# A hybrid decoder trunk: the normalized operands move to another pool, and every attention score product contracts over all 128 partitions

## The chip, the cores and the metric

The kernel runs on one core of one Trainium2 chip. The metric is the device time of one execution in microseconds. Three executions of the kernel before the change gave a median of 1401.86 us, with 1396.67 us the lowest and 1404.54 us the highest.

## What is computed

Two transformer-like layers work on 512 tokens of width 1024. Layer 0 projects its input with one weight matrix for two groups of heads: four retention heads (RetNet) and eight sparse attention heads (NSA) in two key/value groups. The attention has a compressed branch (31 compressed keys), a selected branch and a window branch. With 512 tokens there are eight blocks of 64 tokens and eight are selected, and the window is 512, so both of the latter see every earlier token. Layer 1 is a gated linear recurrence (HGRN2). Each layer ends with a SwiGLU feed-forward network of width 2816. The part that the change touches is cut from the reference here:

```python
def block(i):
    ...
    s_c = jnp.einsum('bghqd,bgnd->bghqn', qb, k_cmp) * scale
    p_c = masked_softmax(s_c, cmp_end[None, :] <= t[:, None])
    ...
    s_s = jnp.einsum('bghqd,bgqkd->bghqk', qb, kg) * scale
    p_s = masked_softmax(s_s, (kpos <= t[None, None, :, None])[:, :, None])
    ...
    s_w = jnp.einsum('bghqd,bgkd->bghqk', qb, kw) * scale
    o_w = jnp.einsum('bghqk,bgkd->bghqd', masked_softmax(s_w, valid_w), vw)

for layer in range(DEPTH):
    h = rmsnorm(x, norm_mix_g[layer])
    ...
    h = rmsnorm(x, norm_ffn_g[layer])
    x = x + swiglu(h, ffn_w1[layer], ffn_w3[layer], ffn_w2[layer]).astype(x.dtype)
```

## The kernel before

**Operands in two parts.** Activations lie feature-major: 128 features on the partitions, 512 tokens along the row. A float32 operand is split into a high and a low part of type float32r, and a product is the sum of three: high by high, low by high, high by low. `accumulate` (L121) issues these three as L127, L128 and L129. The weights are split by `load_split` (L104): a DMA brings a raw block, ScalarE casts the high part `whi`, VectorE or GpSimd subtracts for the low part `wlo`. Both sit in the pool `wp`. The norm writes its result as `hh` (high) and `hl` (low), eight tiles of 128 by 512 each (`Norm.operand`, L166), which lie in the pool `main`. Every projection streams `hh` and `hl` past the weights: the tiles `p_a` and `p_b` of the feed-forward networks, `p_r`, `p_rg`, `p_nq` and others in layer 0, `p_hf`, `p_hq`, `p_hi`, `p_hg` in layer 1. The second half of a feed-forward network (tile `y`) streams `gh` and `gl`, which lie in the pool `big`; so do the operands of the output projections (tile `mo`).

**Attention.** For a head, the query tile `QA` holds the high part on the 64 partitions of its group and the low part on the other 64. The key's high part is kept on both halves (`KA`), so one product over 128 rows (L443) gives high by high plus low by high. The key's low part lies in `KB` only on the group's own 64 partitions, and a second product over these 64 rows (L444) adds high by low. A third, of bf16 (L445), adds the causal mask:

```python
mm(s_[:, 0:n], QA[g][t][:, qs], KA[:, 2 * br + g, 0:n], start=True, stop=False)
mm(s_[:, 0:n], QA[g][t][b, qs], KB[br][b, 0:n], start=False, stop=False)
mm(s_[:, qs], identb, cmaskb, start=False, stop=True)
```

Here `b` is the group's half and `n` is 128, 256, 384 or 512, by the block of queries. There are 64 such triples. The compressed branch does the same with 32 columns (L400 with `kca`, L401 with `kcb` over 64 rows), 32 pairs in four runs of eight (function `nsa`). VectorE then takes the row maximum from PSUM (L446), ScalarE the exponential (L449), GpSimd scales (L456), TensorE transposes (L466), ScalarE and VectorE split the result, and TensorE multiplies by the values (L473, L474).

**Order.** The steps of the attention and of the retention heads are put in one list by `weave` (L56), so that projections `p_r` stand between the attention's products, and scores are issued two steps ahead of the values that use them. The framework's scheduler then settles the order on each engine; each engine runs its own instructions in that order and waits for semaphores.

Of the kernel before, what the change touches and what calls it, by code (L numbers as in the profile page):

```python
# [11 lines left out]
F32 = mybir.dt.float32  # L12
FR = mybir.dt.float32r
# [3 lines left out]
ALU = mybir.AluOpType  # L17
# [3 lines left out]
S = 512  # L21
D = 1024
KT = D // 128
# [8 lines left out]
def trunk(ctx, tc, t_in, out):  # L32
# [22 lines left out]
    # Sequences of steps (matrix time, step) in one, each spread evenly over a span of the whole.  # L55
# [12 lines left out]
    # Residual stream, feature-major.  # L68
    xall = main.tile([128, KT, S], F32, name="xall")
    xT = [xall[:, k, :] for k in range(KT)]  # L70
    hh = [main.tile([128, S], FR, name=f"hh{k}") for k in range(KT)]
    hl = [main.tile([128, S], FR, name=f"hl{k}") for k in range(KT)]
# [28 lines left out]
    # Weights: one block of K-tiles, split exactly into two float32r parts.  # L101
# [35 lines left out]
    # The same in four steps, the last of which hands the sums on.  # L137
# [17 lines left out]
    # RMSNorm: operands x*g; the row factor is applied where products are read.  # L155
# [97 lines left out]
    # ---------------------------------------------------------------- layer 0  # L253
    n0 = Norm(0)
    w0 = t_in["w_in0"]
    # Attention operands in two float32r parts. Per head, a query's halves lie on the two halves
    # of the partitions, beside a key's high part twice; a value's halves lie side by side.
# [3 lines left out]
    KB = [cell(4 + br, f"kb{br}", FR) for br in range(2)]  # L261
# [30 lines left out]
    # kc, vc with token pairs on the partitions: [(j2, d), group, token]  # L292
# [7 lines left out]
    for br in range(2):  # L300
        kf = temp(f"kf{br}")
        nc.vector.tensor_tensor(out=kf, in0=first[2 + br], in1=R0, op=ALU.mult)
        for g in range(2):
            b = slice(g * 64, g * 64 + 64)
            ka = KA[:, 2 * br + g, :]
            for h in range(2):
                nc.scalar.copy(ka[h * 64:h * 64 + 64], kf[b])
            nc.vector.tensor_tensor(out=KB[br][b], in0=kf[b], in1=ka[b].bitcast(F32), op=ALU.subtract)
# [12 lines left out]
    # Compressed keys and values.  # L321
    kca = main.tile([128, 2, 32], FR, name="kca")
    kcb = main.tile([128, 32], FR, name="kcb")
    vc = main.tile([96, 2, 128], FR, name="vc")
    for z in (kca.rearrange("p g n -> p (g n)"), kcb, vc.rearrange("p g d -> p (g d)")):
        nc.scalar.activation(out=z, in_=ones[:z.shape[0], 0:1].to_broadcast(list(z.shape)), func=AF.Copy, scale=0.0)
    for s in range(2):
# [22 lines left out]
        if s == 0:  # L350
            mm(po[:, 0:62], cw2[:, 0:128], u, start=True, stop=True)
            for g in range(2):
                b, src = slice(g * 64, g * 64 + 64), po[:, g * 31:g * 31 + 31]
                nc.scalar.copy(kca[:, g, 0:31], src)
                nc.vector.tensor_tensor(out=kcb[b, 0:31], in0=src[b], in1=kca[b, g, 0:31].bitcast(F32),
                                        op=ALU.subtract)
        else:
            for g in range(2):
                mm(po[:31, g * 64:g * 64 + 64], u[:, g * 31:g * 31 + 31], cw2[:, 128:192], start=True, stop=True)
            src = po[:31, 0:128].rearrange("p (g d) -> p g d", g=2)  # L360
            for r in (0, 32):
                nc.scalar.copy(vc[r:r + 31, :, 0:64], src)
            nc.vector.tensor_tensor(out=vc[64:95, :, 0:64], in0=src, in1=vc[0:31, :, 0:64].bitcast(F32),
                                    op=ALU.subtract)
# [21 lines left out]
    # NSA attention.  # L386
# [3 lines left out]
    def nsa(i):  # L390
# [4 lines left out]
        for g in range(2):  # L395
            b = slice(g * 64, g * 64 + 64)
            sc = bank("sc", f"sc{i}_{g}")
            for t in range(4):
                o = sc[:, t * 32:t * 32 + 32]
                mm(o, QA[g][t][:, qs], kca[:, g, :], start=True, stop=False)  # L400
                mm(o, QA[g][t][b, qs], kcb[b, :], start=False, stop=True)  # L401
            nc.vector.tensor_tensor(out=pc[:, g * 4:g * 4 + 4, 0:31],
                                    in0=sc[:, 0:128].rearrange("p (h n) -> p h n", h=4)[:, :, 0:31],
                                    in1=cmpmask[:, i:i + 1, 0:31].to_broadcast([128, 4, 31]), op=ALU.add)
# [28 lines left out]
    def nsa_scores(i, g, tp, br):  # L433
        n = (i + 1) * 128
        qs = slice(i * 128, n)
        b = slice(g * 64, g * 64 + 64)
        st = small.tile([128, 8], F32, name=f"st{i}_{g}{tp}_{br}", tag="st", bufs=4)
        Ps = []
        for x in range(2):
# [4 lines left out]
            mm(s_[:, 0:n], QA[g][t][b, qs], KB[br][b, 0:n], start=False, stop=False)  # L444
# [37 lines left out]
    # Steps of two heads and a branch; later steps' scores run ahead of a step's values.  # L482
# [27 lines left out]
    # RetNet.  # L510
# [126 lines left out]
    # ---------------------------------------------------------------- layer 1  # L637
# [7 lines left out]
    # Lower bound of the forget gate: a running sum of a softmax over the odd layers, less its  # L645
    # first term, over the single odd layer.
# [45 lines left out]
    def hgrn_mix(h):  # L692
# [6 lines left out]
        # Products over d of a token with itself and with its nearest neighbours, summed by ones.  # L699
# [83 lines left out]
        # The scale of q, 1/sqrt(128), is taken into eps: o is sqrt(128) times the reference's.  # L783
# [24 lines left out]
    # Projections in order, one a beat; each head's recurrence runs beside the next heads'.  # L808
# [44 lines left out]
def _layout(i):  # L853
# [37 lines left out]
    # Constants of the shapes.  # L891
# [34 lines left out]
```

## Time and profile before

The profiled execution spans 1400.5 us from its first to its last instruction, 1.4 us below the median of the three timed ones.

| What | Before |
|---|---|
| median of 3 executions | 1401.86 us |
| span of the profiled execution | 1400.5 us |
| TensorE (PE) busy | 1378.0 us, 98% |
| VectorE (DVE) busy | 718.9 us, 51% |
| ScalarE (ACT) busy | 529.3 us, 38% |
| GpSimd (POOL) busy | 375.5 us, 27% |
| mean granted TensorE clock | 0.985 of full |
| HBM traffic | 83 GB/s over the span |

How to read it: a busy share counts the time in which at least one instruction of the engine is under way. Products on TensorE overlap, since one begins while the one before it still drains, so a product's own duration is longer than the time it costs. What it costs is the distance from its start to the next one's start.

### The profile page before, as it was taken

Reading aid. Unit: us, or ns where it says so; the run is one execution under the profiler, and the core shown is the slowest. Engines: PE = TensorE matmul, PEld = TensorE weight load, DVE = VectorE, ACT = ScalarE, POOL = GpSimd, SP = SyncE. Lnnn points to the kernel's source line nnn. Section 1 sums busy time; section 2 is a strip of 40 time slices with the busy share of each in tenths; the row PEclk is TensorE's granted clock in tenths of the full one; section 3 lists DMA queues with packets and bytes.
Section 4 is the critical chain, followed back from the end, with each engine's and each line's share of the span. In section 5 each row is a group of like instructions: output and inputs, shape, how many; then the busy total and the mean of one; then the engine's idle time right before and its main releaser. Section 6 shows DMA issues by size and latency. Waiting matters only on the chain.

```text
span 1400.5 us, 17591 instructions
## 1 busy us (share of the span) xinstructions
PE 1378.0 (98%) x6591; PEld 1120.4 (80%) x6591; DVE 718.9 (51%) x1261; ACT 529.3 (38%) x982; POOL 375.5 (27%) x383
## 2 busy tenths in 40 slices
PE   7999999999999999999999999999999999999996
PEld 5777778788888888888888888888788888888886
DVE  5744575675343334443438877775743433334333
ACT  5444564644333322333434333332433322233342
POOL 3013556532111000111118656661211110011112
PEclk9998899999999999999999999999999999999998
DMA  6231011103233234333332222222233323323332
GB/s 217 76 91 46 31 31 32 45 18 115 81 102 92 83 100 134 90 91 92 97 98 76 76 61 61 74 62 69 82 92 92 103 83 97 107 92 90 87 91 79
DMA packets 38774, 116.71 MB, mean 83 GB/s; under 512 B 4833, under 2 KB 11169, under 8 KB 38561
## 3 DMA queue, kind: packets, MB, share of 16 engines
q1 hardware_dynamic: 38688, 115.58, 27.6%
q8 instruction: 52, 0.85, 0.3%
q14 instruction: 34, 0.27, 0.1%
HBM read 113.47 MB, written 2.10 MB: 83 GB/s over the span
## 4 chain that ended last, share of the span: by engine, by line
PE 97%; DVE 1%; issue 0%; ACT 0%; DMA 0%; POOL 0%; SPq 0%; DVEq 0%; ACTq 0%; POOLq 0%
PE p_b L129 6%; PE p_b L127 6%; PE p_a L128 6%; PE p_a L127 6%; PE p_b L128 6%; PE p_a L129 6%; PE y L127 6%; PE y L128 6%; PE y L129 6%; PE mo L127 2%; PE mo L128 2%; PE lv L741 2%; PE mo L129 2%; PE p_r L127 2%; PE p_r L128 2%; PE p_r L129 2%
## 5 line engine op out<-in xcount | busy, mean ns | idle before, releaser
L248 POOL TENSOR_TENSOR g<-g,R 128x512 f32<-128x512 f32 x44 | 70.2, 1596 | 535.0 <-DVE g L247 525.4
L129 PE MATMUL p_b<-hh,wlo_b 128*128 128x512 f32 x352 | 139.7, 397 | 0.0
L127 PE MATMUL p_a<-hh,whi_a 128*128 128x512 f32 x352 | 139.7, 397 | 0.0
L127 PE MATMUL p_b<-hh,whi_b 128*128 128x512 f32 x352 | 139.7, 397 | 0.0
L128 PE MATMUL p_a<-hl,whi_a 128*128 128x512 f32 x352 | 139.7, 397 | 0.0
L128 PE MATMUL p_b<-hl,whi_b 128*128 128x512 f32 x352 | 139.5, 396 | 0.0
L129 PE MATMUL p_a<-hh,wlo_a 128*128 128x512 f32 x352 | 139.5, 396 | 0.0
L127 PE MATMUL y<-gh,whi_y 128*128 128x512 f32 (+1 forms) x363 | 139.0, 383 | 0.4 <-DVE xall L223 0.4
L128 PE MATMUL y<-gl,whi_y 128*128 128x512 f32 (+1 forms) x363 | 138.3, 383 | 0.0
L129 PE MATMUL y<-gh,wlo_y 128*128 128x512 f32 (+1 forms) x363 | 138.2, 383 | 0.0
L116 DVE TENSOR_TENSOR wlo_y<-raw_y,whi_y 128x512 fp32r<-128x512 f32 (+1 forms) x96 | 62.6, 653 | 95.2 <-ACT whi_y L114 95.2
L114 ACT CAST whi_y<-raw_y 128x512 fp32r<-128x512 f32 (+1 forms) x96 | 56.4, 587 | 145.8 <-PE y L128 101.9
L116 DVE TENSOR_TENSOR wlo_b<-raw_b,whi_b 128x512 fp32r<-128x512 f32 x88 | 62.7, 713 | 92.8 <-ACT whi_b L114 92.7
L114 ACT CAST whi_b<-raw_b 128x512 fp32r<-128x512 f32 x88 | 54.8, 622 | 135.6 <-issue 61.9
L114 ACT CAST whi_a<-raw_a 128x512 fp32r<-128x512 f32 x88 | 54.6, 620 | 104.5 <-PE p_b L128 71.9
L180 POOL TENSOR_TENSOR acc<-acc,sq 128x512 f32<-128x512 f32 x30 | 41.8, 1394 | 151.9 <-ACT sq L179 151.3
L127 PEld LDWEIGHTS y<-gh,whi_y 128*128 128x128 f32 x363 | 68.2, 188 | 13.9 <-DVE xall L223 0.5
L129 PEld LDWEIGHTS p_a<-hh,wlo_a 128*128 128x128 f32 x352 | 66.3, 188 | 16.1
L129 PEld LDWEIGHTS p_b<-hh,wlo_b 128*128 128x128 f32 x352 | 66.3, 188 | 16.1
L128 PEld LDWEIGHTS p_b<-hl,whi_b 128*128 128x128 f32 x352 | 66.3, 188 | 16.1
L127 PEld LDWEIGHTS p_b<-hh,whi_b 128*128 128x128 f32 x352 | 66.3, 188 | 16.0
L128 PEld LDWEIGHTS p_a<-hl,whi_a 128*128 128x128 f32 x352 | 66.3, 188 | 16.0
(364 smaller groups left out, 3111.7 us busy)
## 6 DMA issues: line engine op xcount, KB each, us to landing
raw_a<-w SPq DMA_DIRECT2D x44, 512.0 KB, 3.6
raw_b<-w SPq DMA_DIRECT2D x44, 512.0 KB, 3.6
raw_y<-w SPq DMA_DIRECT2D x32, 512.0 KB, 3.5
raw_mo<-w_out SPq DMA_DIRECT2D x16, 512.0 KB, 3.6
raw_r<-w_in SPq DMA_DIRECT2D x12, 512.0 KB, 3.7
raw_y<-w SPq DMA_DIRECT2D x32, 192.0 KB, 2.4
raw_hf<-w_in SPq DMA_DIRECT2D x8, 512.0 KB, 3.6
raw_hq<-w_in SPq DMA_DIRECT2D x8, 512.0 KB, 3.6
```

The source lines that it names most:

```text
L114: nc.scalar.copy(hi[:, :m], part)
L116: lo_eng[c // 512 % len(lo_eng)].tensor_tensor(out=lo[:, :m], in0=part, in1=hi[:, :m].bitcast(F32), op=ALU.subtract)
L127: mm(o, wh, xh, start=first and j == 0, stop=False)
L128: mm(o, wh, xl, start=False, stop=False)
L129: mm(o, wl, xh, start=False, stop=last and j == n - 1)
L180: nc.gpsimd.tensor_tensor(out=self.acc, in0=self.acc, in1=sq, op=ALU.add)
L248: nc.gpsimd.tensor_tensor(out=g, in0=g, in1=R, op=ALU.mult)
L741: mm(s_[:M, c * 64:(c + 1) * 64].rearrange("p (a b) -> p a b", b=B), k[:, c * 128:c * 128 + M], q4[:, c * nb:(c + 1) * nb, 1, :], start=Tr ...
```

## The change

`hh` and `hl` are allocated from the pool `wp`, ahead of the weights' tiles, with one buffer each. `KB` becomes one slab of four 128 by 512 tiles (one for each branch and group), filled on both halves of the partitions by four subtractions for a branch instead of two; `kcb` likewise gets one 128-row tile for each group. L444 and L401 then contract over all 128 rows, and so add low by low as well. The scratch that the framework keeps at the start of each partition for DMA descriptors shrinks from 16384 to 4096 bytes. Comments are dropped, so lines shift by one to four: L400 and L401 become L403 and L404, L443 to L445 become L445 to L447, L308 becomes L310, L127 to L129 become L128 to L130.

```diff
-    hh = [main.tile([128, S], FR, name=f"hh{k}") for k in range(KT)]
-    hl = [main.tile([128, S], FR, name=f"hl{k}") for k in range(KT)]
+    hh = [wp.tile([128, S], FR, name=f"hh{k}", tag=f"hh{k}", bufs=1) for k in range(KT)]
+    hl = [wp.tile([128, S], FR, name=f"hl{k}", tag=f"hl{k}", bufs=1) for k in range(KT)]
...
-    KB = [cell(4 + br, f"kb{br}", FR) for br in range(2)]
+    KB = slab(4, "kb", FR)
...
-            nc.vector.tensor_tensor(out=KB[br][b], in0=kf[b], in1=ka[b].bitcast(F32), op=ALU.subtract)
+            for h in range(2):
+                nc.vector.tensor_tensor(out=KB[h * 64:h * 64 + 64, 2 * br + g, :], in0=kf[b],
+                                        in1=ka[b].bitcast(F32), op=ALU.subtract)
...
-    kcb = main.tile([128, 32], FR, name="kcb")
+    kcb = main.tile([128, 2, 32], FR, name="kcb")
...
-                nc.vector.tensor_tensor(out=kcb[b, 0:31], in0=src[b], in1=kca[b, g, 0:31].bitcast(F32),
+                nc.vector.tensor_tensor(out=kcb[:, g, 0:31], in0=src, in1=kca[:, g, 0:31].bitcast(F32),
                                         op=ALU.subtract)
...
-                mm(o, QA[g][t][b, qs], kcb[b, :], start=False, stop=True)
+                mm(o, QA[g][t][:, qs], kcb[:, g, :], start=False, stop=True)
...
-            mm(s_[:, 0:n], QA[g][t][b, qs], KB[br][b, 0:n], start=False, stop=False)
+            mm(s_[:, 0:n], QA[g][t][:, qs], KB[:, 2 * br + g, 0:n], start=False, stop=False)
...
-    nc = _bacc.Bacc("TRN2", target_bir_lowering=False, num_devices=1)
+    nc = _bacc.Bacc("TRN2", target_bir_lowering=False, num_devices=1, dynamic_dma_scratch_size=4096)
```

The pools lie one behind the other in each partition, so tiles of different pools need not start on the same grid. In the two programs as built, the first tile of a kind starts at this byte of the partition (tiles of a kind follow at multiples of 2048):

| Tile | Before | Rest by 64 | After | Rest by 64 |
|---|---|---|---|---|
| `hh` | 32896 | 0 | 31072 | 32 |
| `whi`, `wlo` | 76000 | 32 | 63840 | 32 |
| `gh`, `gl` (first slab) | 121056 | 32 | 108896 | 32 |

The order on SP and GpSimd stays the same. On the other engines it moves in one place, where layer 0's keys and values are made. On VectorE, before (`kb` is the keys' low part, `vf` a value projection ahead of its transposes, `vv` the values' two parts, `wlo_nq` a low part of weights):

```order
L308 TENSOR_TENSOR kb_144<-kf_377,ka 64x512 x2
L308 TENSOR_TENSOR kb_145<-kf_385,ka 64x512
L313 TENSOR_TENSOR vf_428<-p_v_393,R_279 128x512
L308 TENSOR_TENSOR kb_145<-kf_385,ka 64x512
L116 TENSOR_TENSOR wlo_nq_0_608<-raw_nq_604,whi_nq_0_606 128x512
L116 TENSOR_TENSOR wlo_nq_512_612<-raw_nq_604,whi_nq_512_610 128x512
L116 TENSOR_TENSOR wlo_nq_0_649<-raw_nq_645,whi_nq_0_647 128x512
L313 TENSOR_TENSOR vf_472<-p_v_437,R_279 128x512
```

The same place on VectorE in the changed kernel:

```order
L310 TENSOR_TENSOR kb<-kf_376,ka 64x512 x4
L310 TENSOR_TENSOR kb<-kf_386,ka 64x512 x2
L316 TENSOR_TENSOR vf_431<-p_v_396,R_278 128x512
L310 TENSOR_TENSOR kb<-kf_386,ka 64x512 x2
L117 TENSOR_TENSOR wlo_nq_0_611<-raw_nq_607,whi_nq_0_609 128x512
L117 TENSOR_TENSOR wlo_nq_512_615<-raw_nq_607,whi_nq_512_613 128x512
L117 TENSOR_TENSOR wlo_nq_0_652<-raw_nq_648,whi_nq_0_650 128x512
L316 TENSOR_TENSOR vf_475<-p_v_440,R_278 128x512
```

Three more subtractions stand ahead of the first `vf`, and four more ahead of the second.

On TensorE at the same place, before (`h` is the compressed keys' first layer, `vt` the transposes of `vf`):

```order
L338 MATMUL h_0_487<-xkv_488,cw_0_154 64x62 x4
L316 MATMUL vt_430<-ident,vf_428 128x128 x4
L338 MATMUL h_0_487<-xkv_488,cw_0_154 64x62 x4
L338 MATMUL h_0_487<-xkv_499,cw_1_155 64x62 x6
L316 MATMUL vt_474<-ident,vf_472 128x128 x4
```

The same place on TensorE in the changed kernel:

```order
L342 MATMUL h_0_490<-xkv_491,cw_0_153 64x62 x8
L342 MATMUL h_0_490<-xkv_502,cw_1_154 64x62
L319 MATMUL vt_433<-ident,vf_431 128x128 x4
L342 MATMUL h_0_490<-xkv_502,cw_1_154 64x62 x7
L128 MATMUL p_ng<-hh_74,whi_ng_569 32x512
```

The first group of transposes stands five products later, and the second 25 products later: behind the last two of `h` and 23 of the 24 products of `p_ng`.

## Rows read from the trace of the kernel before

**Rows 1.** The page: busy time of each engine, and the chain that ended last.
```profile
PE 1378.0 (98%) x6591; PEld 1120.4 (80%) x6591; DVE 718.9 (51%) x1261; ACT 529.3 (38%) x982; POOL 375.5 (27%) x383
PE 97%; DVE 1%; issue 0%; ACT 0%; DMA 0%; POOL 0%; SPq 0%; DVEq 0%; ACTq 0%; POOLq 0%
```

**Rows 2.** Sums by stretch: stretch, its us, busy us of engines, clock, DMA share, GB/s.
```profile
534.92:658.62 123.70, 123.70 (x530) 99.45 (x528) 50.53 (x77) 39.45 (x65) 16.03 (x10) 1.00 0.32 95
475.06:534.92 59.86, 59.86 (x265) 49.56 (x264) 21.07 (x33) 14.78 (x26) 1.62 (x1) 1.00 0.37 112
```

**Rows 3.** The same view, whole span, instructions on hh alone, then on hl alone.
```profile
0.00:1401.00 1401.00, 762.76 (x2352) 444.27 (x2352) 30.30 (x32) 23.11 (x32) 0.99 0.28 83
0.00:1401.00 1401.00, 471.95 (x1176) 222.92 (x1176) 30.30 (x32) 0.99 0.28 83
```

**Rows 4.** One line's instructions, L444 and L401: count, duration, first and last start.
```profile
L444 PE MATMUL s<-kb,qa x64: 322/438/686, 111.1 to 291.3; 64*128 64x128 f32 x16, 64*128 64x256 f32 x16, 64*128 64x384 f32 x16, 64*128 64x512 f32 x16
...
L401 PE MATMUL sc<-kcb,qa x32: 280/280/393, 107.4 to 220.2; 64*128 64x32 f32 x32
```

**Rows 5.** Waits: engine, line, released by: us in total, times, longest us.
```profile
PEld s L444 <- issue: 10.2, 42, 0.4
```

**Rows 6.** Timeline of TensorE: start, us, instruction; a score triple at n = 512.
```profile
272.41 0.48 PE L443 MATMUL s<-ka,qa 128*128 128x512 f32 x1
272.82 0.49 PE L444 MATMUL s<-kb,qa 64*128 64x512 f32 x1
273.25 0.23 PE L445 MATMUL s<-cmaskb,identb 128*128 128x128 bf16 x1
```

**Rows 7.** Timeline of TensorE, a score triple at n = 128.
```profile
123.59 0.30 PE L443 MATMUL s<-ka,qa 128*128 128x128 f32 x1
123.82 0.32 PE L444 MATMUL s<-kb,qa 64*128 64x128 f32 x1
124.08 0.23 PE L445 MATMUL s<-cmaskb,identb 128*128 128x128 bf16 x1
```

**Rows 8.** Timeline of TensorE, products over all rows behind the mask, and four transposes.
```profile
118.81 0.23 PE L445 MATMUL s<-cmaskb,identb 128*128 128x128 bf16 x1
118.85 0.48 PE L128 MATMUL p_r<-hl,whi_r 128*128 128x512 f32 x1
119.16 0.22 PE L443 MATMUL s<-ka,qa 128*128 128x128 f32 x1
...
285.58 0.60 PE L466 MATMUL pt<-ident,P 128*128 128x128 f32 x4
285.94 0.48 PE L443 MATMUL s<-ka,qa 128*128 128x512 f32 x1
```

**Rows 9.** Timeline of TensorE, the compressed branch's narrow products.
```profile
171.53 0.28 PE L401 MATMUL sc<-kcb,qa 64*128 64x32 f32 x1
171.74 0.28 PE L400 MATMUL sc<-kca,qa 128*128 128x32 f32 x1
171.95 0.28 PE L401 MATMUL sc<-kcb,qa 64*128 64x32 f32 x1
```

**Rows 10.** Sums by stretch: three at the lower clock, and the whole attention stage.
```profile
110.36:117.19 6.83, 6.83 (x20) 5.12 (x20) 2.27 (x8) 1.35 (x4) 0.00 (x0) 0.50 0.00 0
134.26:147.91 13.65, 13.65 (x49) 10.85 (x49) 7.41 (x27) 5.62 (x19) 4.53 (x8) 0.50 0.01 2
219.59:226.42 6.83, 6.83 (x24) 5.61 (x24) 3.97 (x13) 2.22 (x7) 3.19 (x4) 0.50 0.00 0
107.00:296.00 189.00, 188.42 (x990) 146.87 (x989) 114.46 (x294) 100.75 (x250) 95.12 (x106) 0.93 0.12 37
```

**Rows 11.** The chain that ended last, in order of time, where it leaves TensorE: start, us.
```profile
272.95 1.03 DVE st L454
...
274.12 1.05 POOL P L456
275.17 0.56 issue
```

**Rows 12.** One line's instructions, L308: count, shortest/median/longest ns, first and last start.
```profile
L308 DVE TENSOR_TENSOR kb<-kf,ka x4: 669/686/690, 46.1 to 48.8; 64x512 fp32r<-64x512 f32 x4
```

More of the change, by code (lines that the diff above doesn't have):

```diff
@@ L322, in trunk @@
     kca = main.tile([128, 2, 32], FR, name="kca")
-    kcb = main.tile([128, 32], FR, name="kcb")
+    kcb = main.tile([128, 2, 32], FR, name="kcb")
     vc = main.tile([96, 2, 128], FR, name="vc")
-    for z in (kca.rearrange("p g n -> p (g n)"), kcb, vc.rearrange("p g d -> p (g d)")):
+    for z in (kca.rearrange("p g n -> p (g n)"), kcb.rearrange("p g n -> p (g n)"),
+              vc.rearrange("p g d -> p (g d)")):
         nc.scalar.activation(out=z, in_=ones[:z.shape[0], 0:1].to_broadcast(list(z.shape)), func=AF.Copy, scale=0.0)
@@ L352, in trunk @@
             for g in range(2):
-                b, src = slice(g * 64, g * 64 + 64), po[:, g * 31:g * 31 + 31]
+                src = po[:, g * 31:g * 31 + 31]
                 nc.scalar.copy(kca[:, g, 0:31], src)
-                nc.vector.tensor_tensor(out=kcb[b, 0:31], in0=src[b], in1=kca[b, g, 0:31].bitcast(F32),
+                nc.vector.tensor_tensor(out=kcb[:, g, 0:31], in0=src, in1=kca[:, g, 0:31].bitcast(F32),
                                         op=ALU.subtract)
@@ L395, in nsa @@
         for g in range(2):
-            b = slice(g * 64, g * 64 + 64)
             sc = bank("sc", f"sc{i}_{g}")
@@ L435, in nsa_scores @@
         qs = slice(i * 128, n)
-        b = slice(g * 64, g * 64 + 64)
         st = small.tile([128, 8], F32, name=f"st{i}_{g}{tp}_{br}", tag="st", bufs=4)
```

## The prediction

> **What bounds the kernel now.** I read the page first: TensorE is busy 98% of the span and the chain that ended last runs through it for 97% [rows 1]. Every other engine has idle time, so a change pays where it shortens the distance from one product's start to the next one's, or takes a wait from TensorE. The next view is the one of sums by stretch, because busy shares cannot show what a product costs. The second half of the first feed-forward network has a pure stretch of `p_a`/`p_b`, whose moving operands are `hh` and `hl`, and the first half ends with a pure stretch of `y`, which streams `gh` and `gl`. Counted by weight loads (one for each product), the first has 528 products in 123.70 us, 234.3 ns each, and the second 264 in 59.86 us, 226.7 ns each [rows 2]. All are 128 by 512 products over 128 rows, at the full clock and without a gap; DMA moves 95 and 112 GB/s, so the faster stretch has more traffic, not less. Something about `hh` and `hl` costs 7.5 ns a product. In the attention stage I read the timeline. A score triple at 512 columns has its starts at 272.41, 272.82 and 273.25: the 128-row L443 takes 0.41 us to the next start and the 64-row L444 takes 0.43 [rows 6], where a plain product of that size takes 0.23. At 128 columns the same two take 0.23 and 0.26 [rows 7], while four transposes of 128 columns take 0.36, or 0.09 each [rows 8]. The weight load of L444 is the one that the view of waits lists as held, 10.2 us over 42 times, with no releaser named [rows 5]: it does not slip under the product before it, as the others do. Last I looked at the clock: three stretches of 6.83, 13.65 and 6.83 us have a granted clock of 0.50, 1.2 GHz instead of 2.4 [rows 10]. Each begins within a run of the compressed branch's narrow products or right at its end; the last of these starts is at 220.2 [rows 4].
>
> **The moving operands.** 2352 products read `hh` and 1176 read `hl` [rows 3], 3528 in all. At 7.5 ns that is 26.5 us if they come to cost what `gh` and `gl` cost, and 0 if they do not. What tells the two kinds apart is where their tiles start: `hh` is a multiple of 64 bytes, the weights and `gh` are 32 past one. The change puts all of them 32 past, as the table of starts in the section on the change shows. A loss is excluded as far as that remainder counts, since `gh` already has it. I take the whole 26.5 us, since the row of `y` is the nearest one: same shape, same weights' pool, same TensorE work, tile start as it will be. All of this time is on the path, as PE has no gap in these stretches.
>
> Against this part speaks a rule. Whichever tiles TensorE reads, the page "SBUF — State Buffer" of the Trainium skill (section "Who interferes with whom") says that TensorE has separate read ports for the moving operand and the weights and never waits on anyone. By it a change of pool gives 0. The rows do not fit it easily, since two stretches that differ in what they stream differ by 3%, but they do not show the cause either; it is the first rival below.
>
> **The score products.** There are 64 of L444, 16 at each of four widths [rows 4]. At 512 columns L443 and L444 take 0.84 us together [rows 6]. As two full products they would take 0.31 and 0.23: the first figure is what the product behind a mask product takes in rows 8 (118.85 to 119.16), where its weights could not be loaded under the short mask product. That saves 0.30 us. At 128 columns they take 0.49 [rows 7]; two products at the transposes' 0.09, and 0.08 for standing behind the mask, make 0.26, which saves 0.23. The mean, 0.265, times 64 is 17.0 us. For the compressed branch each narrow product takes 0.21 to the next [rows 9]; 32 pairs [rows 4]. At the transposes' 0.09 to at most 0.12 a pair takes 0.22 instead of 0.42, 0.20 saved, 6.4 us in all. Between them 23.4 us. The lower bound is 0, if a 128-row product behind another costs what the 64-row one does; a loss is excluded, since L443 has 128 rows already and is the shorter of the two.
>
> One more rule of the Trainium skill says just that. The page "TensorE: Matmul & The Clock Gate" (section "Why this matters for your kernels") has a single product over 32 rows take the same time as one over 128. By it the sum would lose these 23.4 us. The rows give 0.43 against 0.23 at 512 columns, so here I follow the trace.
>
> **The clock.** The low stretches sum to 27.3 us [rows 10]; at the full clock their work takes half, so 13.7 us is what they cost. With the narrow products at half their spacing and the score products closer together, TensorE streams more columns in the same time right where the clock fell. I take the 13.7 us as gained; the bound on the other side is 0, if all three remain.
>
> **What is given back.** The attention stage takes 189.0 us, of which VectorE is busy 114.5, ScalarE 100.8 and GpSimd 95.1 [rows 10]. Less 23.4, 13.7 and about 2 of its `p_r` products, TensorE would need 150 us, and VectorE would be busy 76% of it instead of 61%. Already now the chain leaves TensorE at 272.95 for 1.03 us of VectorE, 1.05 of GpSimd and 0.56 of issue before the next scores [rows 11]: L443 of a later step needs a buffer that these free. I expect two or three more such waits, 6 us. Between bounds of 0 and 20 (waits of that size, 2.6 us, in each of the eight blocks of steps), I stay nearer the low one because VectorE still has a quarter of the stage idle.
>
> **What is added.** VectorE gets four more subtractions of 0.686 us [rows 12], three of them ahead of `vf`, which the first transposes L316 need: `vf` comes 2.1 us later. The scheduler has put these transposes five products later, some 0.4 us, so up to 1.7 us of wait is left; at most all four show, 2.7 us, and at least none. I take 1. The two subtractions for `kcb` have the same 31 columns on more partitions, and ScalarE's zeroing has 64 elements instead of 32: nothing. Low by low adds no instruction. The smaller DMA scratch changes no issue: SP's order is the same. That is also why the move past `vf` delays no weight load.
>
> **Sum.** 26.5 + 17.0 + 6.4 + 13.7 gained is 63.6; less 6 and 1 is 56.6. From the profiled span of 1400.5 that leaves 1343.9. The median of the runs shown stands 1.4 above that span, so the forecast is **1345 us**, 4% less.
>
> **Rivals.**
> *Only the attention gains.* The remainder of the tiles' start is not what costs 7.5 ns; `hh` and `hl` still lie below the weights, as before, and stay at 234 ns. For it: the view shows two kinds of products, not a cause, and the skill's rule would have it so. Against: nothing else in rows 2 differs in the right direction. 1345 + 26.5 is 1372.
> *The stage becomes bound by others.* VectorE's and GpSimd's chains then end last, waits eat the 13.7 and some 10 of the 23.4, so only 14 of the attention's gain remain instead of 30: 1361. For it: the excursion in rows 11. Against: VectorE's 114.5 us in 150.
> *Slower than before: the clock.* TensorE's new waits fall between the narrow products, and the lower clock holds for far longer. Each us at 1.2 GHz costs half a us of work. Without the gain of the moving operands, the attention's 23.4 us are used up when low stretches rise from 27.3 to 74 us; at 110 us it is 1402 - 23 + 41 = 1420 us. With the moving operands' gain it needs 127 us of low clock to lose. Against: the stage of 189 us had 27 at a spacing that was worse.
> *The change does not do what it says.* The 128-row products cost what the 64-row ones did, and only the operands gain: no score saving and the clock as now, 1402 - 26.5 + 1 = 1376.
>
> **Chances.** The forecast with all its parts has 0.60, and its own range is 1330 to 1358. Only the attention gains: 0.20. Bound by others: 0.12. No score saving: 0.05. Slower by the clock: 0.03. The 1330 takes nothing given back (1338), and some 8 us for plain products that come still closer. The range of 8 in 10 reaches up to 1374, so it takes in the first two rivals whole and leaves out the last two and the tails. About 0.5%, 7 us, is what a measurement of this kernel can tell from no change. By that bound faster gets 0.94, the same 0.03 and slower 0.03.
>
> **What would show it.** In the profile after, the pure stretch of `p_a`/`p_b` should hold 528 products in 119.7 us, and `y` should stay at 59.9. If `p_a` stays at 123.7, the first part is wrong. L445 (once L443) should start 0.31 or less before L446 at 512 columns, and L446 about 0.23 before the mask product; the narrow products should stand 0.11 apart; the held weight loads of L444 should be gone from the waits. The attention stage should show a clock of 1.00 throughout and take about 156 us; if a 0.50 stretch remains, that term is too high. If VectorE or GpSimd appear in the chain for more than some 8 us in that stage, the given-back term is too small. A gain in the hundreds of ns outside these places would mean that I missed a cause.

## The result and the profile after

The changed kernel takes 1349.23 us (median of four executions, 1348.43 to 1349.68), the kernel before 1401.98 us in the same comparison (four, 1396.67 to 1404.54). The ratio is 0.9619, with a 95% interval of 0.9596 to 0.9642. The forecast was 1345. The profiled execution spans 1347.0 us where 1343.9 was forecast, so the change brought 53.5 us of the expected 56.6. One kernel below, with only the pool moved, had a slow execution of 4717.5 us beside three of 1374.04 to 1378.96; the trace kept of it is of the slow one, so its numbers are those of the three and no row of its trace is used.

The page after, busy time and chain, against [rows 1]. TensorE is busy for 56 us less and has 25.4 us without work where it had 22.5.

```profile
PE 1321.6 (98%) x6591; PEld 1101.9 (82%) x6591; DVE 720.0 (53%) x1265; ACT 527.8 (39%) x982; POOL 375.5 (28%) x383
PE 78%; POOL 1%; DVE 1%; ACT 0%; issue 0%; DVEq 0%; POOLq 0%; ACTq 0%
```

The fall of the chain's share from 97% to 78% is no sign of a new bound. This time the chain could be followed back only to 240.2 us, so it says nothing of the stretch before. I read the stages by sums instead.

The view of sums by stretch after the change: the second half layer `p_a`/`p_b`, the `y` stretch ahead of it (against [rows 2]), and the attention from the first compressed score to the last score product. The columns are those of [rows 2].

```profile
497.07:616.75 119.68, 119.68 (x529) 99.13 (x528) 50.57 (x77) 39.44 (x65) 16.07 (x10) 1.00 0.32 97
437.23:497.07 59.84, 59.84 (x265) 49.57 (x264) 21.08 (x33) 14.78 (x26) 1.61 (x1) 1.00 0.37 114
105.51:257.19 151.68, 148.63 (x955) 126.51 (x953) 109.17 (x286) 96.09 (x243) 94.21 (x105) 1.00 0.15 46
```

The 528 products now take 226.7 ns each, as those of `y` do, which have not moved. The attention runs at a clock of 1.00 throughout in this execution. The same stretch of the kernel before:

```profile
107.33:290.85 183.52, 182.94 (x954) 142.31 (x952) 109.85 (x287) 97.45 (x243) 94.11 (x105) 0.93 0.13 38
```

It became 31.84 us shorter. TensorE's time without work within it went from 0.58 to 3.05 us.

The timeline of TensorE after (start, us, instruction): a score triple at n = 512, one at n = 128, and narrow products, against [rows 6], [rows 7] and [rows 9].

```profile
244.07 0.50 PE L445 MATMUL s<-ka,qa 128*128 128x512 f32 x1 [0.36 <-ACT P L451]
244.41 0.40 PE L446 MATMUL s<-kb,qa 128*128 128x512 f32 x1
244.65 0.23 PE L447 MATMUL s<-cmaskb,identb 128*128 128x128 bf16 x1
...
107.21 0.31 PE L445 MATMUL s<-ka,qa 128*128 128x128 f32 x1
107.35 0.28 PE L446 MATMUL s<-kb,qa 128*128 128x128 f32 x1
107.47 0.23 PE L447 MATMUL s<-cmaskb,identb 128*128 128x128 bf16 x1
...
105.76 0.26 PE L404 MATMUL sc<-kcb,qa 128*128 128x32 f32 x1
105.87 0.26 PE L403 MATMUL sc<-kca,qa 128*128 128x32 f32 x1
105.98 0.26 PE L404 MATMUL sc<-kcb,qa 128*128 128x32 f32 x1
```

At 512 columns the two score products stand 0.34 and 0.24 ahead of their followers (before 0.41 and 0.43), at 128 columns 0.14 and 0.12 (before 0.23 and 0.26), and the narrow ones 0.11 apart (before 0.21).

The waits after, of weight loads between 100 and 270 us and of products between 105 and 258, where [rows 5] had the held load of L444. The columns are those of [rows 5].

```profile
PEld L447 <- issue: 6.0, 29, 0.3
PE s L445 <- ACT P L451: 1.4, 3, 0.8
PE vt_rv L290 <- DVE rv L287: 0.5, 1, 0.5
PE oT L475 <- DVE Pl L154: 0.4, 1, 0.4
PE pt L468 <- POOL P L458: 0.4, 1, 0.4
```

The load of `kb` is not among them. It was not the only one held before: the loads of the mask product (L445, now L447) were held too, for 6.7 us over 31 times, and still are:

```profile
PEld L445 <- issue: 6.7, 31, 0.3
```

The products' own waits are four rows, 2.7 us in all; before the change there were two, 0.4 us and 0.2 us.

### The profile page after: what moved, and what is told of

The parts are those of the page before. It is cut to its first block, busy times and chain, and to the rows that moved or that the text cites. A ratio compares the mean times of both kernels' runs of the same rounds, so it can differ in the third digit from the quotient of the medians.

```text
span 1347.0 us, 17596 instructions
## 1 busy us (share of the span) xinstructions
PE 1321.6 (98%) x6591; PEld 1101.9 (82%) x6591; DVE 720.0 (53%) x1265; ACT 527.8 (39%) x982; POOL 375.5 (28%) x383
## 4 chain that ended last, share of the span: by engine, by line
PE 78%; POOL 1%; DVE 1%; ACT 0%; issue 0%; DVEq 0%; POOLq 0%; ACTq 0%
PE y L128 6%; PE p_b L128 6%; PE p_a L129 6%; PE p_b L130 6%; PE y L129 6%; PE p_a L128 6%; PE y L130 6%; PE p_b L129 6%; PE p_a L130 6%; PE mo L128 2%; PE mo L129 2%; PE mo L130 2%; PE lv L743 2%; PE p_hg L129 1%; PE p_hg L130 1%; PE p_hg L128 1%
## 5 line engine op out<-in xcount | busy, mean ns | idle before, releaser
L128 PE MATMUL y<-gh,whi_y 128*128 128x512 f32 (+1 forms) x363 | 139.0, 383 | 0.4 <-DVE xall L224 0.4
L129 PE MATMUL y<-gl,whi_y 128*128 128x512 f32 (+1 forms) x363 | 138.3, 383 | 0.0
L130 PE MATMUL y<-gh,wlo_y 128*128 128x512 f32 (+1 forms) x363 | 138.2, 383 | 0.0
L128 PE MATMUL p_a<-hh,whi_a 128*128 128x512 f32 x352 | 137.1, 390 | 0.0
L130 PE MATMUL p_b<-hh,wlo_b 128*128 128x512 f32 x352 | 137.1, 390 | 0.0
L129 PE MATMUL p_a<-hl,whi_a 128*128 128x512 f32 x352 | 137.1, 390 | 0.0
L128 PE MATMUL p_b<-hh,whi_b 128*128 128x512 f32 x352 | 137.1, 389 | 0.0
L130 PE MATMUL p_a<-hh,wlo_a 128*128 128x512 f32 x352 | 137.0, 389 | 0.0
L129 PE MATMUL p_b<-hl,whi_b 128*128 128x512 f32 x352 | 137.0, 389 | 0.0
L128 PEld LDWEIGHTS y<-gh,whi_y 128*128 128x128 f32 x363 | 68.2, 188 | 13.8 <-DVE xall L224 0.5
L130 PEld LDWEIGHTS y<-gh,wlo_y 128*128 128x128 f32 x363 | 68.2, 188 | 13.4
L129 PEld LDWEIGHTS y<-gl,whi_y 128*128 128x128 f32 x363 | 68.2, 188 | 13.3
L130 PEld LDWEIGHTS p_a<-hh,wlo_a 128*128 128x128 f32 x352 | 66.1, 188 | 13.8
L130 PEld LDWEIGHTS p_b<-hh,wlo_b 128*128 128x128 f32 x352 | 66.1, 188 | 13.7
L128 PEld LDWEIGHTS p_a<-hh,whi_a 128*128 128x128 f32 x352 | 66.1, 188 | 13.6
```

The source lines that it names most:

```text
L128: mm(o, wh, xh, start=first and j == 0, stop=False)
L129: mm(o, wh, xl, start=False, stop=False)
L130: mm(o, wl, xh, start=False, stop=last and j == n - 1)
```

## The experiments

My theory after the result was the prediction's own: `hh` and `hl` gained because their start's rest by 64 bytes now equals that of the weights and of `gh`; the scores gained because of 128 rows; the clock stayed up because the products around the narrow ones stand closer. The rivals were that the pool or another property of the place counts, and that the attention's gain comes from the clock or one of its two parts alone. In all diffs, lines with - and + are those of the kernel named.

**One part at a time.** First only the pool moves (from the kernel before), then all but the pool (from the changed kernel).

```diff
-    hh = [main.tile([128, S], FR, name=f"hh{k}") for k in range(KT)]
-    hl = [main.tile([128, S], FR, name=f"hl{k}") for k in range(KT)]
+    hh = [wp.tile([128, S], FR, name=f"hh{k}", tag=f"hh{k}", bufs=1) for k in range(KT)]
+    hl = [wp.tile([128, S], FR, name=f"hl{k}", tag=f"hl{k}", bufs=1) for k in range(KT)]
```

> The kernel before with only hh and hl moved to the weights' pool; score products over 64 rows as before, DMA scratch as before. hh then starts at byte 43232 (rest 32 by 64), weights stay at 76000 (rest 32). My theory (the remainder of the tiles' starts): the 528 products of a pure p_a/p_b stretch take 119.7 us instead of 123.7, y stays at 59.9, the attention stage keeps its low clock and gains 2 us at most; about 1378 us in all, a ratio of 0.983. Rival (the pool and the place count for nothing, the change's gain in p_a came with the shift of everything else): 123.7 us, 1402 us.

Measured: 1375.82 us, the median of three, against 1400.23, ratio 0.9828 (0.9798 to 0.9857), about 24 us. What `p_a`/`p_b` take with this pool is shown by the changed kernel, where `hh` and the weights stand equally far apart.

The second, with the reverse diff in the changed kernel:

> The changed kernel with hh and hl back in the main pool (start 20608, rest 0; weights 63840, rest 32). My theory: p_a/p_b stretch back at 123.7 us, attention stage near 153.5 us (151.7 measured in the changed kernel plus 2 for its p_r products) at a clock of 1.00, about 1373 us in all, ratio 0.979. Rival (the shorter scratch or the shift of all tiles made the products faster, not the pool): p_a/p_b stays at 119.7 us and the time near 1350 us.

Measured: 1368.00 us, ratio 0.9767 (0.9742 to 0.9791). Sums by stretch, `p_a`/`p_b`:

```profile
503.56:626.76 123.20, 123.20 (x529) 98.97 (x528) 50.53 (x77) 39.35 (x65) 16.10 (x10) 1.00 0.31 95
```

Without the move of the pool these products take 233.3 ns. The attention stage, first compressed score to last score product, and a stretch at the lower clock within it:

```profile
106.57:260.27 153.70, 151.06 (x954) 127.89 (x952) 109.02 (x286) 96.14 (x243) 94.22 (x105) 0.99 0.15 46
127.51:130.92 3.41, 3.41 (x20) 3.41 (x20) 2.48 (x10) 1.88 (x8) 0.46 (x2) 0.50 0.00 0
```

The stage takes 2.0 us more than after the whole change, but most of that is this stretch, not the 288 products of `p_r`: these take 239.9 ns each at the full clock, against 235.5 after the change, which is 1.3 us. So the two parts are separate, and each brings about what the sum gave it. But 233.3 is not the 234.3 of before, though the rest by 64 bytes had gone back to 0. That was the first sign against the cause I had named.

**The cause: unused bytes between the tiles.** In the kernel before, 32 unused bytes ahead of `hh` and 32 behind `hl`, so that all starts have a rest of 32 by 64:

```diff
+    pad0 = main.tile([128, 8], F32, name="pad0")
     hh = [main.tile([128, S], FR, name=f"hh{k}") for k in range(KT)]
     hl = [main.tile([128, S], FR, name=f"hl{k}") for k in range(KT)]
+    pad1 = main.tile([128, 8], F32, name="pad1")
```

> The kernel before with two unused tiles of 32 bytes, one ahead of hh and one behind hl in the main pool: hh starts at 32928 (rest 32), weights at 76064 (rest 32), hh stays in the main pool. The start's remainder, relative to the weights or absolute: p_a/p_b 119.7 us, about 1378 us. Rival (it is the pool, or the place in the partition, that counts): 123.7 us, 1402 us.

Measured: 1394.39 us in one execution. The 528 products:

```profile
529.95:653.14 123.19, 123.19 (x530) 99.12 (x528) 50.43 (x77) 39.38 (x65) 16.03 (x10) 1.00 0.32 95
```

They take 233.3 ns, nearly as before, although every tile has the rest that my theory asked for. **The named cause falls here.** The whole is still 6 us below the kernel before: an estimated 3.5 by 1 ns less for each of 3528 products, and less time at the lower clock in the attention, 20.5 us instead of 27.3. The second kernel has only `pad0`, so that `hh` and the weights both change their rests:

> The kernel before with one unused tile of 32 bytes ahead of hh: hh starts at 32928 (rest 32), weights at 76032 (rest 0), gh and gl at 121088 (rest 0). If what counts is the moving tile's start relative to the weights': p_a/p_b stays slow at 123.7 us and y stays at 59.9, 1402 us. If the moving tile's own remainder counts (32 good, 0 bad): p_a/p_b 119.7 us and y slow at 61.9 (264 by 234.3 ns), about 1402 - 26.5 + 11 = 1387 us.

Measured: 1401.43 us.

```profile
533.93:657.62 123.69, 123.69 (x529) 99.45 (x528) 50.53 (x77) 39.40 (x65) 16.03 (x10) 1.00 0.31 95
474.06:533.93 59.87, 59.87 (x266) 49.57 (x264) 21.07 (x33) 14.76 (x26) 1.62 (x1) 1.00 0.37 113
```

The rests by 64 have changed places, 32 for `hh` and 0 for the weights and `gh`, and nothing moved. In `y` both operands now have a rest of 0 and cost what they did at 32. A place by itself does not count, then; the first of the two expectations held. What this kernel shares with the one before is the distance from the weights' start to that of `hh`: 96 bytes short of a multiple of 256 in both. It is 128 in the kernel with both pads, 32 with the old pool and the new scratch, and 0 after the change.

**The distance, mixed.** Two kernels lay the eight tiles of `hh` (and of `hl`) at eight different distances each, in the hope of a price list from one run:

```diff
-    hh = [wp.tile([128, S], FR, name=f"hh{k}", tag=f"hh{k}", bufs=1) for k in range(KT)]
-    hl = [wp.tile([128, S], FR, name=f"hl{k}", tag=f"hl{k}", bufs=1) for k in range(KT)]
+    off = [0, 8, 16, 32, 48, 64, 96, 112]
+    hha = wp.tile([128, KT * S + 128], FR, name="hha", tag="hha", bufs=1)
+    hla = wp.tile([128, KT * S + 128], FR, name="hla", tag="hla", bufs=1)
+    hh = [hha[:, k * S + off[k]:k * S + off[k] + S] for k in range(KT)]
+    hl = [hla[:, k * S + off[k]:k * S + off[k] + S] for k in range(KT)]
```

> The changed kernel with the eight tiles of hh (and of hl) shifted apart in one larger tile: their starts stand 0, 32, 64, 128, 192, 256, 384 and 448 bytes past the weights' by 512. The two pads have shown that the remainder by 64 is not the whole (equal remainder, 232.9 ns a product). New theory: the distance to the weights' start by 512 bytes sets the price, and 0 is the cheap one: the k-tile at distance 0 near 227 ns, the others 230 to 235. Rival (each distance is alike and only a common distance of all tiles locks into the short beat): all eight near 233. A distance cheaper than 226 would be new.

The second has the offsets 0, 1, 2, 4, 12, 24, 80 and 120 elements of 4 bytes.

> The same with distances of 0, 4, 8, 16, 48, 96, 320 and 480 bytes. New theory: near 227 ns at 0, and a rise to about 234 within some step between 4 and 96 that shows how fine the pattern is. Rival: all eight alike.

Measured: 1362.54 and 1366.35 us; the 528 products in 122.16 and 123.03.

```profile
501.27:623.43 122.16, 122.16 (x530) 99.01 (x528) 50.51 (x77) 39.37 (x65) 16.08 (x10) 1.00 0.31 95
501.69:624.72 123.03, 123.03 (x529) 99.61 (x528) 50.50 (x77) 39.33 (x65) 16.08 (x10) 1.00 0.31 96
```

No price list came of it. By the starts of the products in the first kernel, the tiles average 229.4 to 233.4 ns, the one at distance 0 229.8 and those at 256 and 384 230.0 and 229.4; in the second they average 230.0 to 238.2, the one at 0 232.5. Neither theory nor rival held. So a product's price also hangs on what streams before and behind it, and a distance can be judged only when a whole stretch shares it. These two runs tell that mixing loses, and nothing on single distances.

**One distance for a whole stretch.** The test that decides is the kernel before with nothing but 416 unused bytes, which bring `hh` and the weights to the same start by 512 bytes while each stays in its pool:

```diff
     hl = [main.tile([128, S], FR, name=f"hl{k}") for k in range(KT)]
+    pad = main.tile([128, 104], F32, name="pad")
```

> The kernel before with 416 unused bytes behind hl in the same pool, so that hh, hl and the weights, each still in its old pool, start at the same place counted by 512 bytes (before: 416 apart). Theory, that this distance alone sets what a product costs: the half layers p_a/p_b take 119.7 us as after the change (226.7 ns a product, before 123.7 and 234.3), and the whole time is that of the kernel with only the pool moved, 1377 (1373 to 1381). Rival, that the pool matters in itself (which tile is set up first, or their distance in larger steps, which here stays different from that after the change): 123.2 to 123.7 us and 1394 to 1402.

Measured: 1378.36 us against 1400.86, ratio 0.9833 (0.9804 to 0.9862).

```profile
527.60:647.28 119.68, 119.68 (x529) 99.17 (x528) 50.47 (x77) 39.40 (x65) 16.04 (x10) 1.00 0.32 97
```

The whole gain of the pool's move is there without the move. The next two kernels spoil the changed one: 256 unused bytes behind `hl` and 32 ahead of the pool of `gh`, then 64 and 96.

```diff
     hl = [wp.tile([128, S], FR, name=f"hl{k}", tag=f"hl{k}", bufs=1) for k in range(KT)]
+    pad = wp.tile([128, 64], F32, name="pad", tag="pad", bufs=1)
+    padb = big.tile([128, 8], F32, name="padb", tag="padb")
```

> The changed kernel with an unused tile of 256 bytes between hh/hl and the weights, and one of 32 bytes ahead of gh/gl: hh now start 256 bytes from the weights counted by 512, gh 32. Theory, that only the same start is cheap: p_a/p_b 123 to 123.7 us (119.7 after the change), the y stages 61.3 to 61.9 (59.84), and the whole 1377 to 1383. Rival, that the distance repeats by 256 bytes: p_a/p_b stay at 119.7 and the whole near 1356. Second rival, that small distances cost nothing: y stays at 59.85, the whole near 1371.

> The changed kernel with an unused tile of 64 bytes between hh/hl and the weights, and one of 96 bytes ahead of gh/gl: hh start 64 bytes ahead of the weights, gh 96 behind it, counted by 512. Theory, that only the same start is cheap: p_a/p_b 123 to 123.7 us (119.7 after the change), the y stages 61.3 to 61.9 (59.84), the whole 1377 to 1383. Rival, that whole steps of 64 bytes cost nothing: p_a/p_b stay at 119.7, y rises, the whole near 1357.

Measured: 1359.42 and 1377.10 us. The rows of `p_a`/`p_b` and `y`, of the kernel with 256 and 32 first:

```profile
501.06:620.77 119.71, 119.71 (x529) 99.10 (x528) 50.58 (x77) 39.37 (x65) 16.00 (x10) 1.00 0.31 97
439.45:501.06 61.61, 61.61 (x266) 49.48 (x264) 21.07 (x33) 14.72 (x26) 1.61 (x1) 1.00 0.37 111
```

```profile
505.90:629.10 123.20, 123.20 (x529) 98.74 (x528) 50.58 (x77) 39.32 (x65) 16.12 (x10) 1.00 0.31 94
444.31:505.90 61.59, 61.59 (x265) 49.56 (x264) 21.05 (x33) 14.74 (x26) 1.61 (x1) 1.00 0.35 111
```

My theory held for three of the four distances and fell for 256, where its first rival was right: `p_a`/`p_b` stay at 119.7. All stretches in which one distance rules, by the start of the moving tile less that of the weights, the rest by 256 bytes, each time the stretch by its number of products:

| Rest | Stretch | ns a product |
|---|---|---|
| 0 | `p_a`/`p_b` after; the same with the 416 bytes only; `y` wherever it is not shifted | 226.7 |
| 0 (256) | `p_a`/`p_b`, 256 bytes between | 226.7 |
| 32 | `p_a`/`p_b` with `hh` back in the old pool; `y` at 32 | 233.3; 233.4 |
| 96 | `y` at 96 | 233.3 |
| 128 | `p_a`/`p_b` with `pad0` and `pad1` | 233.3 |
| 160 | `p_a`/`p_b` before; with `pad0` alone | 234.3 |
| 192 | `p_a`/`p_b`, 64 bytes between | 233.3 |

Among the rests tried it is a step and no slope: the same start by 256 bytes, or 3% more. Rests of 64 and 224, and any below 32, were not tried for a whole stretch, and why the distance counts stays open.

**Which weights?** While a product streams, the weights of the next one are loaded (in the kernel before L127 of `p_a` starts at 534.92 us, the load for L128 at 534.93). To see whether the distance to these or to its own counts, 32 bytes go between the high and the low weights, so that `whi` starts where `hh` does and `wlo` where `gh` does:

```diff
+    pads = []
...
             nc.scalar.copy(hi[:, :m], part)
+            if not pads:
+                pads.append(wp.tile([128, 8], F32, name="pad", tag="pad", bufs=1))
             lo = wp.tile([128, 512], FR, name=f"wlo_{name}_{c}", tag="wlo", bufs=5)
```

> The changed kernel with an unused tile of 32 bytes between the weights' high parts and their low parts: whi start where hh and hl do (counted by 256 bytes), wlo and gh/gl start 32 behind. While a product streams, the weights of the next one are loaded. Theory, that the distance to the weights loaded meanwhile counts: in p_a/p_b only L129 (hl by whi, beside the load of wlo) becomes dear, about 233 ns to the next start, with L128 and L130 at 227; in y it is L128 and L130 (beside loads of whi), with L129 at 227. Rival, that the distance to the product's own weights counts: in p_a/p_b L130 is the dear one, in y L128 and L129. Both give some 120.9 us for the p_a/p_b half (119.68), 61.0 for y (59.84) and 1359 in all, by 7 ns for each dear product. Third: if starts within one product do not matter but the change from one to the next does, all three lines rise alike.

Measured: 1376.57 us.

```profile
505.78:628.96 123.18, 123.18 (x530) 99.04 (x528) 50.50 (x77) 39.40 (x65) 16.04 (x10) 1.00 0.30 95
444.20:505.78 61.58, 61.58 (x265) 49.54 (x264) 21.05 (x33) 14.74 (x26) 1.61 (x1) 1.00 0.36 111
```

Both stretches cost as if every product were off, not one or two in three. By the starts in `p_a`/`p_b`, L128 (by the changed kernel's lines) takes 232.0 ns to the next, L129 238.9 and L130 229.0. L129, beside whose streaming the shifted `wlo` is loaded, is the dearest, as the first theory had it, but all three rise. In `y` the order fits neither theory: the three take 236, 233 and 231 ns in the median, so L130, dear by the first theory, is the cheapest, and L129, cheap by it, rises too. Nor does an order by itself tell anything: in `y` at 96, where high and low weights stand at one distance, the three lines take 236.8, 231.1 and 232.0. Which weights count stays open; that one tile off the common start spoils the whole stretch is measured.

**The attention: compressed branch or scores.** From the changed kernel, first the scores go back to 64 rows, then the compressed branch does; the kernel with the 416 bytes has neither part and the same starts. Of each diff only the product is shown; the tile of the low part (`KB`, `kcb`) and its filling go back with it.

```diff
...
-            mm(s_[:, 0:n], QA[g][t][:, qs], KB[:, 2 * br + g, 0:n], start=False, stop=False)
+            mm(s_[:, 0:n], QA[g][t][b, qs], KB[br][b, 0:n], start=False, stop=False)
```

> The changed kernel with the score products L446 back on 64 rows; only the compressed branch's L404 stays on 128. If the low clock came from the long narrow runs, they stay 0.11 us apart and the attention stage has a clock of 1.00 without the 17.0 us of the scores: 151.7 + 17 = 169 us in the stage, about 1366 us. If the spaced score products alone bring the low clock too, one or more stretches at 0.50 remain and each 6.83 us of them adds 3.4: 172 to 182 us in the stage, 1370 to 1380 us.

```diff
...
-                mm(o, QA[g][t][:, qs], kcb[:, g, :], start=False, stop=True)
+                mm(o, QA[g][t][g * 64:g * 64 + 64, qs], kcb[g * 64:g * 64 + 64, :], start=False, stop=True)
```

> The changed kernel with the compressed branch's L404 back on 64 rows; the score products stay on 128. If the low clock came from the narrow runs, three stretches at 0.50 come back: 151.7 + 6.4 + up to 13.7 = 158 to 172 us in the stage, 1356 to 1369 us, near the upper end. If it came from the score products, the clock stays at 1.00 and the stage is 158 us, about 1355 us.

Measured: 1362.85 and 1356.67 us, one execution each. The attention stage by sums, of the kernel with neither, then with the compressed part only, then with the scores only, and of the last one's two stretches at the lower clock:

```profile
103.72:287.46 183.74, 183.16 (x954) 143.86 (x952) 109.08 (x287) 97.40 (x243) 93.94 (x105) 0.92 0.12 38
```

```profile
105.04:270.43 165.39, 164.78 (x954) 129.28 (x953) 110.89 (x287) 97.43 (x243) 94.63 (x105) 1.00 0.14 42
```

```profile
104.07:265.02 160.95, 158.55 (x954) 134.67 (x952) 106.98 (x286) 96.25 (x243) 93.86 (x105) 0.97 0.14 44
...
108.38:111.79 3.41, 3.41 (x10) 2.64 (x9) 1.50 (x6) 0.71 (x3) 0.00 (x0) 0.50 0.00 0
128.86:135.68 6.82, 6.82 (x34) 6.45 (x35) 4.12 (x16) 4.12 (x14) 1.25 (x4) 0.50 0.00 0
```

The kernel with neither has four low stretches in the stage, 30.7 us in all; with the scores only 10.2 us are left, with the compressed part only none. The first expectation for the compressed part held in kind, with the stage 3.6 us below the 169. For the scores, low stretches came back, but two and not three, and the stage is near the lower end of the range and not the upper.

What a low stretch costs is not half of it, as the expectations took it, for work at the lower clock does not take twice as long. Narrow products in a low stretch of the kernel before, against [rows 9]:

```profile
134.64 0.39 PE L400 MATMUL sc<-kca,qa 128*128 128x32 f32 x1
134.96 0.39 PE L401 MATMUL sc<-kcb,qa 64*128 64x32 f32 x1
135.29 0.39 PE L400 MATMUL sc<-kca,qa 128*128 128x32 f32 x1
```

They stand 0.32 us apart instead of 0.21, which is 1.5 times. By the starts, L444 at 128 columns goes from 257 ns to 405, 1.6 times, and a product of `p_r` from 234 to 427, 1.8 times. Compared with the same products between the same neighbours at the full clock, the low stretches took 1.69 times as long in the kernel before, 1.71 with the 416 bytes and 1.81 with the scores only. By these factors the low clock cost an estimated 12.8 us of the 30.7 and 4.6 of the 10.2. Taken out of the stage's time:

| Kernel | Stage, us | Lost to the low clock (estimate) | Rest |
|---|---|---|---|
| neither part | 183.74 | 12.8 | 171.0 |
| compressed part only | 165.39 | 0 | 165.4 |
| scores only | 160.95 | 4.6 | 156.4 |
| both (the change) | 151.68 | 0 | 151.7 |

So the scores bring 13.7 us of work (with the compressed part) to 14.6 (without it), and the compressed part 4.7 to 5.6. The compressed part alone gains 18.4 us, of which 12.8 are the clock's.

How much falls to the low clock varies between executions: in the four traces of kernels with the stage as before it is 20.5, 27.3, 27.3 and 30.7 us, and in the seven with both parts it is none, but for the 3.41 us shown above in the kernel with `hh` in the old pool.

## Why the prediction came out right

The time, the signs of the terms and the order of their sizes were right. One cause was wrong, and four sizes were off. The gains were forecast 7.6 us too high and the losses 3.7 too high, so the errors cancelled in part.

**The moving operands: right in time, wrong in cause.** The step that failed is "What tells the two kinds apart is where their tiles start: `hh` is a multiple of 64 bytes, the weights and `gh` are 32 past one." The rest by 64 tells nothing; the distance between the two starts by 256 bytes does. In the kernel before and in the changed one both readings agree, which is why the forecast held: the change makes all starts equal by 256 bytes, and equal starts have equal rests. That the change made the distance 0 and not only the rests equal was luck as far as the named cause goes: `pad0` and `pad1`, which give the same rests at a distance of 128, parted the two, and there the products gained 1 ns instead of 7.5.

The term was 26.5 us. The move of the pool alone measured 24 (ratio 0.9828), the 416 bytes alone 23 (0.9833), and the intervals hold 26.5; by stages it comes to some 22. In the feed-forward networks the term came whole: 2112 products, 15.8 us less over four half layers, 7.5 ns each. In the recurrence it came by half. Its stage, before and after:

```profile
718.47:964.98 246.51, 246.51 (x1367) 206.92 (x1365) 181.96 (x302) 91.71 (x164) 143.90 (x167) 1.00 0.24 70
```

```profile
676.59:919.85 243.26, 243.11 (x1366) 206.44 (x1365) 180.15 (x302) 91.68 (x164) 143.38 (x167) 1.00 0.23 71
```

That is 3.25 us for 768 products, where 7.5 ns each would be 5.8. TensorE has no gap there before and 0.15 us after. By the starts, the products stand 240.6 ns apart before and 236.4 after, with 312 products `lv` of 64 columns and others strewn among them. The 613 that stand between two of their own kind went from 234.0 to 228.8; the 155 that have another product beside them gained next to nothing, 266.9 to 266.3. The price of [rows 2] is that of a pure stretch, and I carried it into a mixed one. The 288 products of `p_r` in the attention give 1.2 us (239.5 to 235.5 ns at the full clock), and the start of layer 0 is 1.8 us shorter.

**The rule against it**, from the Trainium skill's page "SBUF — State Buffer" (section "Who interferes with whom"), that TensorE never waits on anyone, gives 0 here. The runs show 226.7 against 233 to 234 ns with nothing changed but unused bytes; the measurement decides. The rival on it had a chance of 0.20, too much only in hindsight: at that time no row showed a cause.

**The scores and the compressed branch: the spacing as forecast, a part of it given back.** From the starts, by width and at the full clock, the two score products of 64 triples cost 40.4 us to their followers before and 23.8 after: 16.6 saved, where 17.0 was forecast. The single sizes differ, since L446 has 0.24 at 512 but L445 0.34, and 128 columns gained as forecast. The 32 pairs went from 13.1 to 6.9, 6.2 saved, where 6.4 was forecast. The prediction took the held load of L444 for the only one; that of the mask product was held as well, and is so still, so a held load alone is no mark of 64 rows. The rule of the Trainium skill's page "TensorE: Matmul & The Clock Gate", section "Why this matters for your kernels", would have given nothing: the kernel with the 64-row scores put back is 13.7 us slower in that stage.

**The clock: 13.7 forecast, some 11 found.** No low stretch is left in the stage, as forecast. But "at the full clock their work takes half" was mis-sized: at the factor of 1.69, the 27.3 us of [rows 10] cost an estimated 11.1. That the compressed part alone leaves no low stretch, with the scores still on 64 rows, bears out the rows that began each stretch within the narrow products or at their end. That the scores alone left 10.2 us, where the same stage as before has 20.5 to 30.7, says that the scores around those runs count too. Both rest on one execution each.

**Given back: 6 forecast, some 3.3 found.** The clock's 11.1, 16.6, 6.2 and the 1.2 us of `p_r` make 35.1; the stage fell by 31.8. Of the 3.3, 2.5 us are time without work on TensorE (0.58 to 3.05). The wait in the piece of [rows 11] stood there before and has not grown, 0.36 us. The longest one is new and of the same kind, a score that waits for ScalarE's exponential of an earlier one. The wait of before, then the new one:

```profile
276.56 0.51 PE L443 MATMUL s<-ka,qa 128*128 128x512 f32 x1 [0.36 <-ACT P L449]
```

```profile
158.83 0.45 PE L445 MATMUL s<-ka,qa 128*128 128x384 f32 x1 [0.85 <-ACT P L451]
```

The mask product, which without waits now takes 63 ns to its follower instead of 46, gives back 1.1 us more over 64, and a few others gained a little. Without the 128-row scores the time without work stays at 0.6 us (165.39 less 164.78), with them alone it is 2.4 (160.95 less 158.55), so it is the scores' gain that meets the other engines.

**Added work: 1 forecast, 0 found.** In the kernel with only the compressed part changed, as in that with the 416 bytes alone, the stretches of `p_v` and `p_ng` take 14.6 and 5.6 us; with the added `kb` subtractions they take 14.1 and 6.0. What the later `vf` cost in one place it gave back in the other.

What is left of the 53.5 us lies elsewhere and is under 0.9. Of the rivals, the bound by other engines was nearest in kind, but at some 3 us instead of 24.

## What to carry to other kernels

When two stretches of the same products differ by a few per cent with no gap and less traffic in the slower one, compare the addresses of what is streamed and what is loaded beside it, and test with unused bytes: 416 of them brought 1.7% here. Put moving tiles and weights at the same start by 256 bytes, and all of them, since one shifted kind spoiled the stretch. Look in a mixed stage for short products beside which the clock falls: the compressed branch, some 5 us of work, was worth 18 while the scores were slow. Price a low stretch by the products in it, at both clocks, and not by half.

## What the runs showed of the hardware

- A product of 128 by 512 float32r takes 226.7 ns if its moving tile and the weights start at the same place by 256 bytes, and 233 to 234 at rests of 32, 96, 128, 160 and 192, in a pure stretch. Moving both by 32 changed nothing (123.69 against 123.70 us), nor did the pool (119.68 us in either).
- The price belongs to a stretch. With eight distances mixed, tiles at 0 took 229.8 and 232.5 ns, and with only `wlo` shifted all three kinds of product rose (232.0, 238.9, 229.0).
- A 64-row product between 128-row ones cost 0.43 us to the next start at 512 columns, over all 128 rows 0.24; narrow pairs 0.42 and 0.22.
- At a granted clock of 0.50 (1.2 GHz) the distance between starts grew 1.5 times for the narrow pairs (0.21 to 0.32 us), 1.6 for a 64-row score product of 128 columns (257 to 405 ns) and 1.8 for a full product (234 to 427).
